# A hybrid attention/RWKV-7 layer on one core: the recurrence's chain in program order on TensorE, and 64-row products of two heads in turn

## The chip, the cores and the metric

The kernel runs on one core of a Trainium2 chip. The core has five engines with a queue of instructions each: TensorE (PE in the profile, its weight loads PEld), VectorE (DVE), ScalarE (ACT), GpSimd (POOL) and SyncE (SP, which here issues the DMAs). The metric is the device time of one execution in microseconds (us).

## The reference

The layer takes x of 1024 tokens by 1024 features. One projection of the normalised x feeds two mixers and a gate; the mixers' outputs are joined, gated, projected and normalised again.

```python
u = rmsnorm(h, norm_pre_g[l]);  p = u @ w_in[l]
p_mla, p_rw, z = jnp.split(p, [MLA_COLS, MLA_COLS + RW_SHIFT_COLS], axis=-1)
...                                   # MLA: 4 heads of causal attention, rope, low-rank q and kv -> y_mla
ps = p_rw + (token_shift(p_rw) - p_rw) * rw_mu[l]
r, k, v, xw, xa = jnp.split(ps, ...)  # 8 heads of 64 channels; xw, xa feed tanh/low-rank decay w and rate a
...
def step(S, inp):                     # one token; S is 64x64 per head
    r_t, w_t, k_t, v_t, kk_t, a_t = inp
    sa = jnp.einsum('bhvk,bhk->bhv', S, -kk_t)
    S = (S * w_t[:, :, None, :] + sa[..., None] * (kk_t * a_t)[:, :, None, :]
         + v_t[..., None] * k_t[:, :, None, :])
    return S, jnp.einsum('bhvk,bhk->bhv', S, r_t)
...                                   # group norm of y over each head, bonus -> y_rw
y_cat = jnp.concatenate([y_mla, y_rw], axis=-1) * jax.nn.silu(z)
h = h + rmsnorm(y_cat @ w_out[l], norm_post_g[l])
```

All of it is float32; projections are made of three products of split operands (a high part and a rest).

## The kernel before

**Stages.** A string, PROGRAM, names the stages in the order in which their instructions are created. The 1024 tokens are two halves (h = 0, 1) of 512. `A` loads x, normalises it and makes the transposed, split operand uH/uL (32 transposes of 128x128, L177, each group of four followed by two splits on ACT, L181, and two on DVE, L182). `X` projects the columns of the low-rank inputs (24 matmuls of 512 columns, L210), shifts, takes tanh and splits on DVE into xw and xa (L241 to L244). `P` makes k, r, v and decay of two heads (`P h cb`, cb = 0 to 3; its low-rank products are L250/L251), `E` the units of the chunked recurrence of these two heads, `I` the 64x64 inverses (four rounds of 32x32 products, L447 and L454, with DVE and DMA between), `C` the chain, `N` group norm, `G` the outputs. `Z` are blocks of the gate (24 matmuls of L210 each), `Y06` two of them at once in 96 matmuls of 256 columns; `M`, `T`, `U`, `K`, `J`, `Q` and `S` belong to the attention, `B` to the rope table (DVE, L655 to L676). In the order of PROGRAM, `A1 X1` (input of half 1) come behind the chain of half 0 and its outputs.

**What sets the order.** Each engine runs its queue in order. The queues are filled by a scheduler: it plays the instructions through a model of time, takes on each engine among those whose inputs are there, and gives way to the earlier in the program. So while the chain waits, instructions of later stages come between its steps. A tile taken from a pool holds back an instruction until the pool's oldest buffer is free; PSUM has pools `pj` (4 buffers), `wk` (2) and `ch` (2).

**Units.** A chunk is 64 tokens; a half has 8. Two heads lie on partitions 0 to 63 and 64 to 127. For each head (e = 0, 1) and four chunks, L359 multiplies 64 rows by 64 rows into 128x128 of a `wk` buffer; the same with a diagonal at L373, eight chunks into another `wk` buffer. A float32 matmul stands in the trace as two instructions. Before, `units` writes the L359 products with e as the inner loop, the L373 products head after head, and the scheduler sets the order on TensorE.

**The chain.** Eight steps, one a chunk, each of two groups g of two head pairs. Per group: L474 (four matmuls, eight instructions) state times LS; ACT copies the result out (L476); L480 four more into the same bank; L484 with AB; ACT and DVE copy it (L486, L487) into SV; L490 with BK; DVE adds the decayed state (L494, two of 64x128 a group), which is the state of the next step; L496 adds to the output, which ACT copies out (L499). In each, the four matmuls go over the quarters of the array.

**After the chain** `N` squares, reduces and takes a power on POOL (L510) per group, and `G` transposes the output by head (16 transposes of 64 rows a group, L525).

Of the kernel before, what the change touches and what calls it, by code (L numbers as in the profile page):

```python
# [44 lines left out]
def layer(tc, x, pos, w_in, w_out, w_uq, w_ukv, vecs, w2, a2, consts, post_g, out):  # L45
# [84 lines left out]
    "A0 X0 Z00 B P00 E00 Z01 P01 E01 Z02 P02 E02 P03 E03 I0 C0 N00 G00 N01 G01 M0 Z03 Z04 Z05 Y06 T0 A1 X1",  # L130
    "P10 E10 Z10 P11 E11 Z11 P12 E12 P13 E13 I1 C1 N10 G10 N11 G11 M1 Z12 T1 Z13 Z14 Z15 Z16 Z17 U K J Q0",
# [4 lines left out]
def recurrence(tc, E):  # L136
# [17 lines left out]
    def stage_a(h):

        XT = (("v", "sq"), ("sg", "cs"), ("a", "k"), ("kf", "r"))
        for pr in range(2):
            xs = []
            for q in range(2):
# [8 lines left out]
                E["rstd"](ss[:, 0:1], 1.0 / D)  # L168
# [3 lines left out]
            for k2 in range(4):  # L172
                ps = pj((128, 2, 256))
                for kk in range(2):
                    kb = k2 * 2 + kk
                    for q in range(2):
                        PE.transpose(ps[:, kk, q * 128:(q + 1) * 128], xs[q][kb // 4][:, (kb % 4) * 128:(kb % 4 + 1) * 128], ident)  # L177
                for kk in range(2):
                    kb = k2 * 2 + kk
                    sl = slice(pr * 256, pr * 256 + 256)  # L180
                    S.activation(uH[:, kb, sl], ps[:, kk], AF.Copy, scale=col(V_PRE + kb))  # L181
                    V.scalar_tensor_tensor(uL[:, kb, sl], ps[:, kk], col(V_PRE + kb),  # L182
                                           uH[:, kb, sl].bitcast(F32), ALU.mult, ALU.subtract)
# [19 lines left out]
    def proj(c0):  # L203
# [8 lines left out]
        return ps  # L212
# [22 lines left out]
    def lora_in(h):  # L235
        px = shifted(proj(CO_X), V_MU_X, "v", 1)
# [109 lines left out]
    def units(h, cb, gt, made):  # L346
# [6 lines left out]
        for c4 in range(0, NCH, 4):  # L353
            mk = mks[c4 // 4]
            pE = [wk((128, 4, 128)) for _ in range(2)]
            for ci in range(4):
                for e in range(2):
                    r = slice(e * 64, e * 64 + 64)
                    PE.matmul(pE[e][:, ci], pl[r, c4 + ci, 1 - e:3 - e].rearrange("p a b -> p (a b)"),  # L359
                              LS[r, c4 + ci, e, :], start=True, stop=True)  # L360
# [7 lines left out]
        G.tensor_tensor(dD, bc(id2.unsqueeze(1), (128, NCH, 64)), bc(Dg.unsqueeze(2), (128, NCH, 64)), ALU.mult)  # L368
        for e in range(2):
            r = slice(e * 64, e * 64 + 64)  # L370
            pB = wk((128, NCH, 64))
            for c in range(NCH):
                PE.matmul(pB[:, c], pl[r, c, 1 - e:3 - e].rearrange("p a b -> p (a b)"), dD[r, c], start=True, stop=True)  # L373
# [84 lines left out]
    def chain(h, gt):  # L458
# [4 lines left out]
        for c in range(NCH):  # L463

            pcs = [chp((128, 4, 2, 64)) for _ in range(2)]
            Rs = [alloc(P1, (128, 2, 64), "Rs", bufs=2) for _ in range(2)]
            SD = [alloc(P1, (128, 2, 64), "SD", bufs=2) for _ in range(2)]
            parts = []
            for g in range(2):
                LS, BK, AB, SV = (gt["g"][g][k] for k in ("LS", "BK", "AB", "SV"))  # L470
                parts.append((LS, BK, AB, SV, Sst[:, 2 * g:2 * g + 2], gt["Dg"][:, 2 * g:2 * g + 2], pcs[g], Rs[g], SD[g]))
            for LS, BK, AB, SV, St, Dg, pc, R_, D_ in parts:
                for l, e in le:
                    PE.matmul(pc[ev[e], 0, l], LS[:, l, c, e, 0:64], SV[:, c, e, l], start=(l == 0), stop=False,  # L474
                              skip_group_check=True)
                S.copy(R_, pc[:, 0])  # L476
                for e in range(2):
                    G.tensor_tensor(D_[ev[e]], SV[ev[e], c, e], bc(Dg[ev[e], :, c:c + 1], (64, 2, 64)), ALU.mult)  # L478
                for l, e in le:
                    PE.matmul(pc[ev[e], 1, l], LS[:, l, c, e, 64:128], SV[:, c, e, l], start=False, stop=False,  # L480
                              skip_group_check=True)
            for LS, BK, AB, SV, St, Dg, pc, R_, D_ in parts:
                for l, e in le:
                    PE.matmul(pc[ev[e], 2, l], AB[ev[e], l, c, 0:64], R_[ev[e], l], start=False, stop=False,  # L484
                              skip_group_check=True)
                S.copy(SV[ev[0], c, 0], pc[ev[0], 2])  # L486
                V.tensor_copy(SV[ev[1], c, 1], pc[ev[1], 2])  # L487
            for LS, BK, AB, SV, St, Dg, pc, R_, D_ in parts:
                for l, e in le:
# [571 lines left out]
```

## Time and profile before

| | |
|---|---|
| median of 3 runs | 786.29 us (783.88 to 789.08) |
| profiled execution, own time | 783.81 us |
| its span | 782.0 us |
| mean granted TensorE clock | 0.951 of full |
| DVE busy | 466.4 us (60%) |
| ACT busy | 347.9 us (44%) |
| POOL busy | 331.9 us (42%) |
| L210, all projections, busy | 215.7 us with uH, 130.2 us with uL |
| L359, busy, instructions | 35.6 us, 256 |
| L373, busy, instructions | 31.2 us, 256 |
| L525, busy, instructions | 4.2 us, 64 |

The table is read from the page's summary and from its groups. A matmul's time in a group includes its way through the array, so neighbours overlap: the time that a row of them takes is the distance of their starts. In timelines a row joins neighbours of one kind: start in us, length in us, engine, line, output and inputs, shape, count; a bracket gives the idle time of the engine ahead of it and who ended it. In windows, a row is a stretch: its length, busy time and count of each engine, the granted clock, the share of DMA and GB/s.

### The profile page before, as it was taken

How to read it: one execution, taken by the hardware profiler on the slowest of the kernel's cores; microseconds unless marked ns; L12 is line 12 of the kernel's file. 1: busy time of each engine (PE TensorE's matmuls, PEld its weight loads, DVE VectorE, ACT ScalarE, POOL GpSimd, SP SyncE). 2: the span in 40 equal slices, each digit the busy share in tenths (PEclk: the TensorE clock that was granted, in tenths of full speed). 3: DMA queues.
4: the chain of work that ended last, by engine and by line, in shares of the span. 5: the costliest groups of instructions: out<-in, count | busy, mean ns of one | idle time of the engine just before them, and what ended most of it. 6: DMA issues, size and time to landing. Idle time of an engine off the chain costs nothing. (4 is left out here: it accounts for less than half of the span.)

```text
span 782.0 us, 13855 instructions
## 1 busy us (share of the span) xinstructions
PE 713.0 (91%) x5136; PEld 586.1 (75%) x5136; DVE 466.4 (60%) x943; ACT 347.9 (44%) x877; POOL 331.9 (42%) x478
## 2 busy tenths in 40 slices
PE   2789999999978998889999989799899998899996
PEld 1667877789866776667888967577678997788885
DVE  4756757758925522495866691476497767644333
ACT  6465355343725453344353162426354566632221
POOL 6265645445942554263554374032332237442220
PEclk9999999999998899977999989879999999999999
DMA  6224241254383133043223366411023025144321
GB/s 208 80 69 115 54 114 51 68 151 134 114 187 89 28 108 83 2 89 85 57 68 97 86 171 156 131 44 42 2 55 101 21 89 162 52 166 141 121 82 54
DMA packets 118819, 72.84 MB, mean 93 GB/s; under 512 B 47072, under 2 KB 108256, under 8 KB 118752
## 3 DMA queue, kind: packets, MB, share of 16 engines
q1 hardware_dynamic: 118752, 71.96, 32.5%
q8 instruction: 40, 0.66, 0.4%
q14 instruction: 27, 0.22, 0.1%
HBM read 54.38 MB, written 17.56 MB: 92 GB/s over the span
## 5 line engine op out<-in xcount | busy, mean ns | idle before, releaser
L210 PE MATMUL pj<-uH,w 128*128 128x512 f32 x640 | 215.7, 411 | 3.3 <-DVE uL L182 2.5
L200 POOL TENSOR_TENSOR w<-wf,w 128x256 fp32r<-128x256 f32 x168 | 141.3, 871 | 116.6 <-ACT w L190 106.5
L210 PEld LDWEIGHTS pj<-uH,w 128*128 128x128 f32 x640 | 123.7, 195 | 33.1 <-DVE uL L182 2.9
L210 PE MATMUL pj<-uL,w 128*128 128x512 f32 x320 | 130.2, 407 | 0.0
L210 PEld LDWEIGHTS pj<-uL,w 128*128 128x128 f32 x320 | 62.6, 196 | 14.0 <-issue 0.8
L190 ACT CAST w<-wf 128x1024 fp32r<-128x1024 f32 (+1 forms) x50 | 51.4, 1027 | 28.8 <-PE pj L540 21.3
L478 POOL TENSOR_TENSOR SD<-SV,Dg 64x128 f32<-64x128 f32 x64 | 27.9, 436 | 74.0 <-DVE SV L494 59.9
L854 POOL TENSOR_SCALAR wf<-wf,sm 128x128 f32<-128x128 f32 (+7 forms) x32 | 24.0, 750 | 67.1 <-DVE sm L853 51.9
L198 POOL TENSOR_TENSOR w<-wf,w 128x224 fp32r<-128x224 f32 x32 | 23.8, 775 | 38.8 <-ACT w L190 32.2
L359 PEld LDWEIGHTS wk<-LS,pl 64*128 64x128 f32 x256 | 30.2, 191 | 12.5 <-issue 10.2
L979 DVE TENSOR_TENSOR LS<-pj,LS 128x512 f32<-128x512 f32 x16 | 11.1, 691 | 45.5 <-ACT cq L978 44.3
L359 PE MATMUL wk<-LS,pl 64*128 64x128 f32 x256 | 35.6, 289 | 1.3 <-DVE LS L317 1.2
L850 ACT ACTIVATE wf<-pj,mx 128x512 f32<-128x512 f32 (+3 forms) x48 | 27.7, 583 | 13.5 <-DVE mx L847 9.9
L865 ACT CAST BK<-wk 128x512 fp32r<-128x512 f32 (+3 forms) x48 | 22.4, 485 | 25.2 <-PE wk L863 23.2
L373 PEld LDWEIGHTS wk<-r,pl 64*128 64x128 f32 x256 | 29.5, 196 | 4.4 <-issue 2.9
L373 PE MATMUL wk<-r,pl 64*128 64x64 f32 x256 | 31.2, 284 | 1.2 <-DVE LS L364 1.0
L874 PE MATMUL ch<-BK,LS 128*128 128x256 f32 (+1 forms) x160 | 31.6, 282 | 0.7 <-ACT BK L865 0.7
L487 DVE COPY SV<-ch 64x128 f32<-64x128 f32 x32 | 9.2, 294 | 36.5 <-issue 25.7
L418 DVE TENSOR_TENSOR tmp<-XA 128x31 f32<-128x31 f32 (+15 forms) x62 | 28.2, 454 | 4.4 <-DMA XA<-sa 2.6
L866 DVE TENSOR_TENSOR AB<-wk,BK 128x512 fp32r<-128x512 f32 (+3 forms) x48 | 26.0, 551 | 7.3 <-ACT BK L865 6.8
L420 DVE TENSOR_TENSOR XA<-XA,tmp 128x31 f32<-128x31 f32 (+15 forms) x62 | 28.4, 458 | 1.9
L845 DVE TENSOR_REDUCE mx<-pj 128x1 f32<-128x512 f32 (+3 forms) x48 | 25.8, 551 | 6.0 <-PE pj L844 3.4
(339 smaller groups left out, 1659.4 us busy)
## 6 DMA issues: line engine op xcount, KB each, us to landing
wf<-in_w_in_dram SPq DMA_DIRECT2D x42, 512.0 KB, 3.9
zs<-st SPq DMA_DIRECT2D x16, 256.0 KB, 3.1
wf<-in_x_dram SPq DMA_DIRECT2D x8, 512.0 KB, 3.7
out_dram<-LS SPq DMA_DIRECT2D x16, 256.0 KB, 2.1
wf<-in_w_in_dram SPq DMA_DIRECT2D x8, 448.0 KB, 3.5
bvd<-st SPq DMA_DIRECT2D x8, 256.0 KB, 2.0
SV<-bvd SPq DMA_DIRECT2D x16, 128.0 KB, 3.4
yrw<-SV SPq DMA_DIRECT2D x8, 256.0 KB, 2.6
```

Of the source, the lines that this page charges most:

```text
L190: S.copy(wh, wf)
L200: G.tensor_tensor(wl[:, sl], wf[:, sl], wh[:, sl].bitcast(F32), ALU.subtract)
L210: PE.matmul(ps, w_[:, kb], u_[:, kb], start=(n == 0), stop=(n == 23))
L359: PE.matmul(pE[e][:, ci], pl[r, c4 + ci, 1 - e:3 - e].rearrange("p a b -> p (a b)"), LS[r, c4 + ci, e, :], start=True, stop=True)
L373: PE.matmul(pB[:, c], pl[r, c, 1 - e:3 - e].rearrange("p a b -> p (a b)"), dD[r, c], start=True, stop=True)
L418: V.tensor_tensor(t3, bc(At[:, j, j + 1:32].unsqueeze(2), (128, n, w)), bc(X[:, j, 0:w].unsqueeze(1), (128, n, w)), ALU.mult)
L420: V.tensor_tensor(X[:, j + 1:32, 0:w], X[:, j + 1:32, 0:w], t3, ALU.add)
L478: G.tensor_tensor(D_[ev[e]], SV[ev[e], c, e], bc(Dg[ev[e], :, c:c + 1], (64, 2, 64)), ALU.mult)
L845: V.tensor_reduce(mx[:, n5:n5 + 1], s_, axis=AX.X, op=ALU.min)
L850: S.activation(pr[:, b0:b1], sc[:, 0:b1 - b0], AF.Exp, bias=mx[:, 0:1], scale=-1.0, accum_out=sm[:, n5:n5 + 1])
L866: V.tensor_tensor(PL[:, b0:b0 + nb, o], pt[:, 0:nb], PH[:, b0:b0 + nb, o].bitcast(F32), ALU.subtract)
L874: PE.matmul(py[:, o], l_, r_, start=(j == 0 and n == 0), stop=(j == nk - 1 and n == 2), skip_group_check=True)
```

## The change

1. **Chain.** `chain` takes an iterator `fill`. Inside `tc.manual_schedule` TensorE keeps the program's order: the chain's blocks as written, group 0 before group 1, and one step of `fill` behind the two blocks with AB, one at the end of a step and one more at the end of every second. For half 0, `fill` is `stage_a(1)` and `lora_in(1)` cut into steps (eight of four transposes, then twelve of two matmuls); for half 1 it is empty. `A1 X1` go from PROGRAM.
2. **Order behind a mark.** `tc.issue_after` sets that what is created later on an engine also stands later in its queue: on DVE behind the last split of `A0`, on POOL behind its last power, on TensorE behind the last matmul of `C0`.
3. **64-row products.** In `units` the products of the two heads alternate matmul by matmul on TensorE (new L384, before L359; new L398, before L373, with both `wk` buffers taken at once); so do the transposes of `outputs` (new L558, before L525, two `ch` buffers at once).
4. **PROGRAM.** `M0 Z03 Z04 Z05 T0` move ahead of `C0`, `P10` ahead of `G00`, and `Y06` becomes `Z06 Z07` (48 matmuls of 512 columns).

Line numbers move: 170 to 182, 177 to 189, 181/182 to 194/195, 210 to 223, 250/251 to 274/275, 359 to 384, 373 to 398, 474 to 500, 480 to 506, 484 to 510, 490 to 517, 494 to 521, 496 to 523, 525 to 558, 655/661 to 700/706.

```diff
-        for op in " ".join(PROGRAM).split():
-            name = op.rstrip("0123456789")
-            ops[name](*(int(i) for i in op[len(name):]))
+        with contextlib.ExitStack() as order:
+            for op in " ".join(PROGRAM).split():
+                name = op.rstrip("0123456789")
+                last = ops[name](*(int(i) for i in op[len(name):]))
+                if op in ("A0", "C0"):
+                    for made in last:
+                        order.enter_context(tc.issue_after(made.ins))
...
-    "A0 X0 Z00 B P00 E00 Z01 P01 E01 Z02 P02 E02 P03 E03 I0 C0 N00 G00 N01 G01 M0 Z03 Z04 Z05 Y06 T0 A1 X1",
-    "P10 E10 Z10 P11 E11 Z11 P12 E12 P13 E13 I1 C1 N10 G10 N11 G11 M1 Z12 T1 Z13 Z14 Z15 Z16 Z17 U K J Q0",
+    "A0 X0 Z00 B P00 E00 Z01 P01 E01 Z02 P02 E02 P03 E03 I0 M0 Z03 Z04 Z05 Z06 Z07 T0 C0 N00 N01 P10 G00 G01",
+    "E10 Z10 P11 E11 Z11 P12 E12 P13 E13 I1 C1 N10 G10 N11 G11 M1 Z12 T1 Z13 Z14 Z15 Z16 Z17 U K J Q0",
...
+                if n % 2 == 0:
+                    yield
...
-            for ci in range(4):
-                for e in range(2):
-                    r = slice(e * 64, e * 64 + 64)
-                    PE.matmul(pE[e][:, ci], pl[r, c4 + ci, 1 - e:3 - e].rearrange("p a b -> p (a b)"),
-                              LS[r, c4 + ci, e, :], start=True, stop=True)
+            with tc.manual_schedule(engines={PE.engine}):
+                for ci in range(4):
+                    for e in range(2):
+                        PE.matmul(pE[e][:, ci], pl[ev[e], c4 + ci, 1 - e:3 - e].rearrange("p a b -> p (a b)"),
+                                  LS[ev[e], c4 + ci, e, :], start=True, stop=True)
...
+        pB = [wk((128, NCH, 64)) for _ in range(2)]
+        with tc.manual_schedule(engines={PE.engine}):
+            for c in range(NCH):
+                for e in range(2):
+                    PE.matmul(pB[e][:, c], pl[ev[e], c, 1 - e:3 - e].rearrange("p a b -> p (a b)"), dD[ev[e], c],
+                              start=True, stop=True)
...
-    def chain(h, gt):
+    def chain(h, gt, fill):
...
+        with tc.manual_schedule(engines={PE.engine}):
+            for c in range(NCH):
...
                 S.copy(SV[ev[0], c, 0], pc[ev[0], 2])
                 V.tensor_copy(SV[ev[1], c, 1], pc[ev[1], 2])
+                next(fill, None)
...
                 S.copy(SV[:, c, 0], pc[:, 1])
+                next(fill, None)
+                if c % 2:
+                    next(fill, None)
+            for _ in fill:
+                pass
+        return [mm]
...
+        pT = [chp((128, NCH, 64)) for _ in range(2)]
+        with tc.manual_schedule(engines={PE.engine}):
+            for c in range(NCH):
+                for e in range(2):
+                    PE.transpose(pT[e][:, c], SV[ev[e], c, 0].rearrange("p l v -> p (l v)"), ident[ev[e], ev[e]])
...
+    def op_c(h):
+        return chain(h, gts[h], itertools.chain(stage_a(1), lora_in(1)) if h == 0 else iter(()))
```

The first place is TensorE in a late step of the chain of half 0. Before (`ch` with two numbers are the PSUM tiles of the two groups):

```order
L474 MATMUL ch_2053<-SV_363,LS_360 64x64 x4
L474 MATMUL ch_2054<-SV_367,LS_364 64x64 x4
L480 MATMUL ch_2053<-SV_363,LS_360 64x64 x4
L484 MATMUL ch_2053<-Rs_2055,AB_362 64x64 x4
L480 MATMUL ch_2054<-SV_367,LS_364 64x64 x4
L484 MATMUL ch_2054<-Rs_2056,AB_366 64x64 x4
L490 MATMUL ch_2053<-SV_363,BK_361 64x64 x4
L490 MATMUL ch_2054<-SV_367,BK_365 64x64 x4
L496 MATMUL ch_2053<-SV_363,AB_362 64x64 x4
L496 MATMUL ch_2054<-SV_367,AB_366 64x64 x4
```

The same step in the changed kernel (the two `L223` rows are steps of `fill`, the projection of `X` for half 1):

```order
L500 MATMUL ch_2638<-SV_363,LS_360 64x64 x4
L506 MATMUL ch_2638<-SV_363,LS_360 64x64 x4
L500 MATMUL ch_2639<-SV_367,LS_364 64x64 x4
L506 MATMUL ch_2639<-SV_367,LS_364 64x64 x4
L510 MATMUL ch_2638<-Rs_2640,AB_362 64x64 x4
L510 MATMUL ch_2639<-Rs_2641,AB_366 64x64 x4
L223 MATMUL pj_2499<-uH_98,w_2493 128x512 x2
L517 MATMUL ch_2638<-SV_363,BK_361 64x64 x4
L523 MATMUL ch_2638<-SV_363,AB_362 64x64 x4
L517 MATMUL ch_2639<-SV_367,BK_365 64x64 x4
L523 MATMUL ch_2639<-SV_367,AB_366 64x64 x4
L223 MATMUL pj_2499<-uL_99,w_2493 128x512
```

Before, a block that waits for another engine's copy has a block of the other group ahead of it. Now the second and the fourth block of a group's turn stand directly behind the first and the third.

The second place is TensorE in `units` of the first two heads. Before:

```order
L210 MATMUL pj_514<-uH_98,w_508 128x512
L359 MATMUL wk_544<-LS_360,pl_431 128x128 x4
L384 MATMUL pj_598<-q_477,cst_64 128x512
L359 MATMUL wk_545<-LS_360,pl_431 128x128 x4
L210 MATMUL pj_620<-uH_98,w_614 128x512
```

And now (the two numbers of `wk` are the two heads; the first product, of `wk_544`, stands seven rows further up, alone between a projection and L411, before L384):

```order
L223 MATMUL pj_629<-uH_98,w_623 128x512
L384 MATMUL wk_545<-LS_360,pl_431 128x128
L384 MATMUL wk_544<-LS_360,pl_431 128x128
L384 MATMUL wk_545<-LS_360,pl_431 128x128
L384 MATMUL wk_544<-LS_360,pl_431 128x128
L384 MATMUL wk_545<-LS_360,pl_431 128x128
L384 MATMUL wk_544<-LS_360,pl_431 128x128
L384 MATMUL wk_545<-LS_360,pl_431 128x128
L223 MATMUL pj_629<-uH_98,w_623 128x512
```

Two rows of four products of one head have become seven products that change heads each time, and one that stands alone.

The third place is DVE at the start (`uL` is the split of `A0`, `posf` and `q` the rope table, `kf` and `r` two tiles of x). Before:

```order
L182 SCALAR_TENSOR_TENSOR uL_99<-pj_146,vec_65,uH_98 128x256
L661 TENSOR_SCALAR q_330<-cst_64,posf_327 128x32 x5
L170 TENSOR_SCALAR kf_178<-kf_178,ss_42_180 128x512
L170 TENSOR_SCALAR r_179<-r_179,ss_42_180 128x512
L661 TENSOR_SCALAR q_330<-cst_64,posf_327 128x32 x2
L182 SCALAR_TENSOR_TENSOR uL_99<-pj_155,vec_65,uH_98 128x256
```

And now, first where x's last tiles stand:

```order
L195 SCALAR_TENSOR_TENSOR uL_99<-pj_128,vec_65,uH_98 128x256
L195 SCALAR_TENSOR_TENSOR uL_99<-pj_137,vec_65,uH_98 128x256
L182 TENSOR_SCALAR kf_178<-kf_178,ss_42_180 128x512
L182 TENSOR_SCALAR r_179<-r_179,ss_42_180 128x512
L195 SCALAR_TENSOR_TENSOR uL_99<-pj_146,vec_65,uH_98 128x256
```

Then where the table begins:

```order
L195 SCALAR_TENSOR_TENSOR uL_99<-pj_201,vec_65,uH_98 128x256
L195 SCALAR_TENSOR_TENSOR uL_99<-pj_219,vec_65,uH_98 128x256
L195 SCALAR_TENSOR_TENSOR uL_99<-pj_210,vec_65,uH_98 128x256
L195 SCALAR_TENSOR_TENSOR uL_99<-pj_219,vec_65,uH_98 128x256
L700 CAST posf_327<-posi_325 128x8
L706 TENSOR_SCALAR q_330<-cst_64,posf_327 128x32 x8
```

The table's rows stood between x's last tiles and their splits, and stand behind all splits now.

More of the change, by code (lines that the diff above doesn't have):

```diff
@@ L1 @@
+import contextlib
+import itertools
 import math
@@ L57, in rstd @@
         G.tensor_scalar(ss, ss, scale, EPS, ALU.mult, ALU.add)
-        G.tensor_tensor(ss, ss, mhalf[:, 0:ss.shape[-1]], ALU.pow)
+        return G.tensor_tensor(ss, ss, mhalf[:, 0:ss.shape[-1]], ALU.pow)
     def bc(ap, shape):
@@ L149, in col @@
         return vec[:, c:c + 1]
+    ev = (slice(0, 64), slice(64, 128))
+    le = [(l, e) for l in range(2) for e in range(2)]
     uH = alloc(P1, (128, 8, HALF), "uH", F32R)
     uL = alloc(P1, (128, 8, HALF), "uL", F32R)
+    last = [None, None]
     def stage_a(h):
@@ L167, in stage_a @@
                 G.tensor_tensor(ss[:, 0:1], ss[:, 0:1], ss[:, 1:2], ALU.add)
-                E["rstd"](ss[:, 0:1], 1.0 / D)
+                last[1] = E["rstd"](ss[:, 0:1], 1.0 / D)
                 for i in range(2):
@@ L211, in proj @@
                 n += 1
-        return ps
+                if n % 2 == 0:
+                    yield
+        out.append(ps)
+    def proj(c0):
+        out = []
+        for _ in proj_steps(c0, out):
+            pass
+        return out[0]
     def shifted(ps, vi, tag, bufs):
@@ L235, in lora_in @@
     def lora_in(h):
-        px = shifted(proj(CO_X), V_MU_X, "v", 1)
+        out = []
+        yield from proj_steps(CO_X, out)
+        px = shifted(out[0], V_MU_X, "v", 1)
         th = alloc(P1, (128, 512), "sq")
@@ L462, in chain @@
                 G.tensor_copy(gt["g"][g]["SV"][ev[e], 0, e], Sst[ev[e], 2 * g:2 * g + 2])
[L463 to L489, printed above, removed]
-                    PE.matmul(pc[ev[e], 3, l], BK[:, l, c, e], SV[:, c, e, l], start=False, stop=False,
-                              skip_group_check=True)
-                for e in range(2):
-                    dst = SV[ev[e], c + 1, e] if c + 1 < NCH else St[ev[e]]
-                    V.tensor_tensor(dst, pc[ev[e], 3], D_[ev[e]], ALU.add)
-                for l, e in le:
-                    PE.matmul(pc[ev[e], 1, l], AB[ev[e], l, c, 64:128], SV[ev[e], c, e, l], start=False,
-                              stop=True, skip_group_check=True)
-                S.copy(SV[:, c, 0], pc[:, 1])
@@ L593, in recurrence, with run, op_a @@
     lora, xx, gts, cqs, made = {}, {}, {}, {}, {}
+    def run(*steps):
+        for _ in itertools.chain(*steps):
+            pass
+    def op_a(h):
+        run(stage_a(h))
+        return last
     def op_x(h):
-        if h == 0:
-            lora_load()
-        xx[h] = lora_in(h)
+        lora_load()
+        run(lora_in(h))
+    def op_c(h):
+        return chain(h, gts[h], itertools.chain(stage_a(1), lora_in(1)) if h == 0 else iter(()))
     def op_p(h, cb):
@@ L611, in recurrence @@
     return {
[L612 to L613 removed]
+        "A": op_a, "X": op_x, "P": op_p, "M": op_m, "T": lambda h: mla_tail(h, cqs[h]),
+        "E": op_e, "I": lambda h: inverse(h, gts[h]), "C": op_c,
         "N": lambda h, g: group_norm(h, g, gts[h]), "G": lambda h, g: outputs(h, g, gts[h]), "Z": lambda h, b: zgate(h, b, b + 1),
```

58 lines of the change are left out of this document (41 added, 17 removed).

## The prediction

> **What bounds the kernel now.** I read the page's summary first, then timelines of TensorE and of all engines in the stages that the change touches, and last TensorE's busy time in windows.
>
> ```profile
> PE 713.0 (91%) x5136; PEld 586.1 (75%) x5136; DVE 466.4 (60%) x943; ACT 347.9 (44%) x877; POOL 331.9 (42%) x478
> ```
>
> TensorE bounds: 713 of 782 us. So three things count: TensorE time taken away, its idle time, and its clock. That 91% is an average, though; the chain differs. This is a step of the chain of half 0 with nothing between its blocks (timeline of all engines, the chain's rows):
>
> ```profile
> 316.19 0.93 PE L474 MATMUL ch<-SV,LS 128*64 128x64 f32 x16
> 316.69 0.27 ACT L476 COPY Rs<-ch 128x128 f32<-128x128 f32 x1
> 317.01 0.45 PE L480 MATMUL ch<-SV,LS 128*64 128x64 f32 x8
> 317.39 0.45 PE L484 MATMUL ch<-Rs,AB 64*64 64x64 f32 x8
> ...
> 318.29 0.29 DVE L487 COPY SV<-ch 64x128 f32<-64x128 f32 x1 [2.53 <-issue]
> 318.64 0.45 PE L490 MATMUL ch<-SV,BK 128*64 128x64 f32 x8
> 319.38 1.21 DVE L494 TENSOR_TENSOR SV<-ch,SD 64x128 f32<-64x128 f32 x4
> 319.40 0.45 PE L490 MATMUL ch<-SV,BK 128*64 128x64 f32 x8 [0.31 <-DVE SV L487]
> 320.02 0.45 PE L496 MATMUL ch<-SV,AB 64*64 64x64 f32 x8 [0.17 <-DVE SV L494]
> 320.64 0.45 PE L496 MATMUL ch<-SV,AB 64*64 64x64 f32 x8 [0.17 <-DVE SV L494]
> 321.02 0.93 PE L474 MATMUL ch<-SV,LS 128*64 128x64 f32 x16
> ```
>
> A step takes 321.02 − 316.19 = 4.83 us. A block of eight instructions takes 317.39 − 317.01 = 0.38, ten of them 3.8, so about 1 us is waiting. The order of the two groups hides most of the copies: while ACT copies group 0's result, L474 of group 1 runs.
>
> **The chain's new order.** Four latencies matter. From L474's start to L480's of the same group, through the copy: 317.01 − 316.19 = 0.82. From L484 to L490 of group 0: 318.64 − 317.39 = 1.25. From L490 to L496: the adds begin 0.55 after it wherever DVE isn't late, two of them take 0.60, the start 0.04: 1.19 (in the rows above 1.38 for group 0, of which 0.2 is DVE's). The new order, block for block from 0: L500 of group 0 at 0, L506 at 0.82; group 1 at 1.20 and 2.02; L510 at 2.40 and 2.78; L517 of group 0 at 2.40 + 1.25 = 3.65, L523 at 4.84; group 1 at 5.22 and 6.41; the next step at 6.79. So the step takes 6.8 us instead of 4.83: L506 of group 0 now waits for its copy with L500 of group 1 queued behind it, L523 of group 0 waits for the add with L517 of group 1 behind. The steps of `fill` behind L510 lie in the 0.49 us before L517; those at a step's end lie on the path.
>
> **The clock.** Windows of 3.41 us (columns: stretch, its length, busy time and count of PE, PEld, DVE, ACT, POOL, granted clock, DMA):
>
> ```profile
> 251.48:254.90 3.42, 1.68 (x39) 1.40 (x40) 2.55 (x4) 2.56 (x9) 2.39 (x3) 1.00 0.00 0
> 254.90:258.31 3.41, 2.51 (x20) 1.92 (x17) 2.21 (x4) 0.81 (x3) 1.20 (x2) 0.50 0.30 61
> 258.31:261.72 3.41, 3.41 (x10) 2.64 (x9) 1.41 (x2) 3.18 (x5) 2.21 (x2) 0.50 0.32 97
> 306.09:309.50 3.41, 2.40 (x54) 1.79 (x48) 1.77 (x4) 1.67 (x7) 3.19 (x6) 1.00 0.03 7
> 323.16:326.57 3.41, 2.22 (x28) 1.96 (x28) 3.28 (x6) 2.01 (x6) 1.14 (x3) 1.00 0.02 5
> 326.57:329.98 3.41, 3.41 (x21) 2.33 (x20) 1.19 (x5) 0.57 (x1) 0.53 (x1) 0.50 0.00 0
> ```
>
> The grid is chosen so that the clock changes at its edges. After 1.68 and after 2.22 us of busy TensorE the next window is at half; after 2.40 it isn't (the step at 316, in the table above, has blocks of 0.38). At half, 2.51 did not bring the clock back. So I put the edge between 2.2 and 2.4 going down and above 2.5 coming up. The new bare step is busy for its 10 blocks and the tails of the five that a wait follows (0.07 each, 0.45 against 0.38), 4.15 us of 6.8, or 2.08 of 3.41: below the edge. At half clock a block takes 0.63:
>
> ```profile
> 503.44 0.69 PE L484 MATMUL ch<-Rs,AB 64*64 64x64 f32 x8
> 504.07 1.06 PE L728 MATMUL wk<-cst,k 128*64 128x128 f32 x4
> ```
>
> That is 0.25 more a block, and nine of them lie on the step's path: 9.04 us, with 10 × 0.63 and tails, 6.7, busy, or 2.54 a window: not enough to come back by the rows above. With `fill` the share is 64%, 2.2 a window.
>
> The Trainium skill ("TensorE: Matmul & The Clock Gate", section "Why this matters for your kernels") asks only that no idle gap of TensorE be over about 3 us. By it the chain, whose waits are all below 1 us, would keep full clock, and the sum would be that of the first rival. This trace speaks against it: the longest wait in the window 323.16 to 326.57 is 1.19, and half clock follows:
>
> ```profile
> 324.62 1.88 PE L359 MATMUL wk<-LS,pl 64*128 64x128 f32 x16 [1.19 <-DVE LS L317]
> ```
>
> **Half 0's chain, old and new.** Before, four steps lie between the projections of half 1 and cost their 3.8, four are bare: 4 × 3.8 + 4 × 4.83 = 34.5. `A1 X1` stand ahead and among them:
>
> ```profile
> 232.02 0.33 PE L177 MATMUL pj<-cst,v 128*128 128x128 f32 x1 [1.47 <-ACT st L565]
> ...
> 242.01 0.33 PE L177 MATMUL pj<-cst,k 128*128 128x128 f32 x1
> ...
> 242.60 0.45 PE L480 MATMUL ch<-SV,LS 128*64 128x64 f32 x8
> ...
> 244.32 0.62 PE L210 MATMUL pj<-uH,w 128*128 128x512 f32 x2
> 244.78 0.39 PE L210 MATMUL pj<-uL,w 128*128 128x512 f32 x1
> ...
> 256.70 0.79 PE L250 MATMUL pj<-xw,lora 128*128 128x512 f32 x1 [0.90 <-DVE xw L242]
> ```
>
> From the end of the work before (232.02 − 1.47) to 256.70 are 26.1 us; 6.1 of them are 16 blocks of the chain, 1.4 a row of L454: 18.6 for `A1 X1` with their waits. Together 53. New: eight steps of 6.8 are 54.4. Of the 20 steps of `fill`, 8 lie in the wait before L517; 12 are on the path: 4 of transposes at 242.60 − 242.01 = 0.59 and 8 of two matmuls at 2 × 0.23: 6. The eight splits' copies stand ahead of the chain's on ACT and DVE, by about one of 0.4 each: 3.3. That is 63.9 at full clock; at half, 9 × 0.25 a step and `fill` doubled, 88.4. I take half clock in six of the eight steps, 82: the first window must go by before the clock falls, and steps with three `fill` pieces may hold it.
>
> After the chain, before:
>
> ```profile
> 337.65 2.91 POOL L510 TENSOR_TENSOR gss<-gss,mhalf 128x16 f32<-128x16 f32 x1
> 338.49 5.81 PE L373 MATMUL wk<-r,pl 64*128 64x64 f32 x32 [1.04 <-DVE LS L364]
> 353.35 1.21 PE L525 MATMUL ch<-cst,SV 64*128 64x64 f32 x16 [4.14 <-DVE SV L513]
> ```
>
> The waits of 4.14, 1.04 and the 1.19 further up are 6.4, and the 32 products of L373 take 5.81 where they took 3.32 at full clock; with some 10 us that half clock costs over the stretch, 16 lost. New, all that is created after `C0` stands behind it. First comes L558, which waits for a copy, square, reduce, the power of 2.91 and two multiplies, 6.8 us by my estimate; then L274 waits for xw, whose splits share DVE with the group norm, until about 10.4; with a window of half clock behind, 12.4. So −4 (−12 to +4). Half 0 in all: 82 − 53 − 4 = +25 (full clock +7, half throughout +31).
>
> **Half 1's chain.** `fill` is empty; by the order of instructions four steps are bare and part of a fifth, before three. Full clock: 4 × 6.8 − 3 × 4.83 − 3.8 = 8.9, and 2 for the part: +11. Three of four at half clock, 2.2 each: +17.6. Attention's work follows at once and TensorE bounds it, so this lies on the path.
>
> **64-row products.** One head's L359 and L373, each with a row behind that gives its length:
>
> ```profile
> 63.55 1.16 PE L359 MATMUL wk<-LS,pl 64*128 64x128 f32 x8
> 64.64 1.12 PE L384 MATMUL pj<-q,cst 128*128 128x512 f32 x2
> ...
> 78.53 3.39 PE L373 MATMUL wk<-r,pl 64*128 64x64 f32 x32
> 81.85 0.72 PE L210 MATMUL pj<-uH,w 128*128 128x512 f32 x2
> ```
>
> 8 take 1.09, 32 take 3.32: 0.104 each. Where the trace has by chance two heads in turn, the starts are 0.05 apart, for one of each head:
>
> ```profile
> 371.77 0.27 PE L359 MATMUL wk<-LS,pl 64*128 64x128 f32 x1
> 371.82 0.27 PE L373 MATMUL wk<-r,pl 64*128 64x64 f32 x1
> ```
>
> So the halves overlap. L359, 256 instructions in 28 pieces: 32.7 us; in turn, 13 pieces of 1 and 7 products and three of 8, at 0.104 alone and about 0.055 in turn, 22.6: −10. L373: 28, to eight pieces of 1 and 15, 2.36 each, 18.9: −9. L525: −1. That is −20 on TensorE, which has no gap in these stages (columns as in the windows above):
>
> ```profile
> 395.00:430.00 35.00, 35.00 (x192) 28.46 (x191) 24.82 (x37) 13.30 (x34) 17.43 (x23) 1.00 0.28 79
> ```
>
> DVE works 24.8 of 35 us there, so a period 2.5 shorter still leaves it time; but `wk` has two buffers and both heads now hold them at once, so I take −17. The bounds are −22 and, if those few rows don't carry over to whole pieces, +3 for the changes of half. `Y06` in two has as many columns in half the instructions; 48 × 0.23 = 11 us and no row says that 96 shorter ones took much more: −0.5 (−1 to 0).
>
> **Start.** The table's rows on DVE lie between x and its splits:
>
> ```profile
> 17.00 3.64 DVE L661 TENSOR_SCALAR q<-cst,posf 128x32 f32<-128x32 f32 x5
> 26.90 0.80 PE L210 MATMUL pj<-uH,w 128*128 128x512 f32 x1 [2.54 <-DVE uL L182]
> 43.63 0.77 PE L250 MATMUL pj<-xw,lora 128*128 128x512 f32 x1 [2.61 <-DVE xw L242]
> ```
>
> Without them the last tiles are scaled 3.6 us earlier and the splits run without gaps. The table then stands ahead of the shift and of xw's splits, which still have to wait for 24 matmuls. I take −4.5 (0 to −6).
>
> **Sum.** 783.8 (own time) − 4.5 − 17 − 0.5 + 25 + 17.6 = 804.4. The median before lies 2.5 above the profiled execution; with it 807. Changes of about 1% (778.4 to 794.2) are what a measurement can tell from none.
>
> **Rivals.** (1) *The clock holds* in both chains, since the waits are short: half 0 +7, half 1 +11, and the sum is 779.8, with the 2.5 782. For it: 2.2 of 3.41 in the steps with `fill` is on the edge. Against: 1.68 and 2.22 were followed by half. A chance of 0.25. (2) *Faster: DVE's late starts vanish.* L487 began 0.35 after TensorE's block was done, by "issue" and no wait, L494 0.29 after; with the groups apart each copy finds an idle DVE. Then a step is 6.79 − 0.35 − 2 × 0.29 = 5.86; busy 2.4 a window, so the clock holds too; half 0 gives 63.9 − 8 × 0.93 − 57 = −0.5, half 1 11 − 5 × 0.93 = 6.4; with all 20 of the products: 783.8 − 4.5 − 20 − 0.5 − 0.5 + 6.4 = 764.7, with the 2.5 767. It decides from a step of about 6.2, where the share passes 2.3. 0.20. (3) *The halves don't overlap* in the written pieces: +3 for −17, 827. 0.05. The forecast keeps 0.50.
>
> **Range.** The forecast alone has 794 to 822 (half clock in fewer steps; all of them, and products at −12). Down to 770 it takes in the first rival and some of the second: outside are 0.15 of that and the third's 0.05. Faster by over 1%: the second, and a fifth of the first, 0.25; within: the rest of the first, some of the forecast's foot, 0.24; slower 0.51.
>
> **What would show it.** Right: rows of L506 and L523 with waits for ACT and DVE, some 0.4 and 0.8 each; windows of half clock across both chains; L398's 0.05 apart; the first L223 before 23 us; the distance of first to last chain row near 82 us in half 0. Wrong: bare steps under 6 us, a clock of 1.00 through the chain, or stalls of `fill` on PSUM or ACT that make its steps longer than 11 us.

## The result and the profile after

The changed kernel takes 821.6 us (median of 4 runs, 813.1 to 826.9) against 785.1 before. The ratio leaves out two of these runs, which were slower at a lower clock, and so is not the quotient of the medians: it is 1.038, with an interval of 1.029 to 1.048. The prediction was 807 us, 770 to 822, slower with a chance of 0.51. The direction and its main reason were right. The measured time stands at the upper end of the range, though: the profiled execution took 817.5 us where the sum without the added 2.5 has 804.4, so about 13 us are missing.

The page's summary of the kernel after, and the rows of its 40 slices for TensorE and its clock:

```profile
PE 704.6 (86%) x5088; PEld 572.8 (70%) x5088; DVE 462.1 (57%) x943; ACT 350.6 (43%) x876; POOL 332.7 (41%) x478
...
PE   3899998999467777999999988597788999899996
...
PEclk9899999999855695999999999697579999999998
```

TensorE has 8 us less busy time in its records and 42 us more idle time (815.7 − 704.6 against 782.0 − 713.0). Two stretches stand out: slices 11 to 16 (from about 204 to 326 us) and 26 to 30 (510 to 612). They are the inverse and the chain of half 0, and those of half 1.

Where the time came in is best read from a few marks, start or end of rows in the timelines of TensorE (us from the span's start):

| | before | after | after − before |
|---|---|---|---|
| first low-rank product (L250, now L274) | 43.6 | 37.2 | −6.4 |
| last product of E03 (L359, now L384) | 172.2 | 168.8 | −3.4 |
| chain of half 0 starts | 236.8 | 236.8 | 0 |
| chain of half 1 starts | 500.1 | 519.2 | +19.1 |
| chain of half 1 ends | 576.8 | 612.5 | +35.7 |
| end | 782.0 | 815.7 | +33.7 |

The start brought TensorE forward by 6.4 us; at the last product of E03 3.4 of it are left, and at the chain of half 0 nothing. From there to the start of half 1's chain the kernel loses 19 us, and in that chain 17; behind it 2 come back.

A step of half 1's chain with nothing between its blocks (timeline of TensorE, kernel after):

```profile
576.00 0.69 PE L500 MATMUL ch<-SV,LS 128*64 128x64 f32 x8
577.06 0.69 PE L506 MATMUL ch<-SV,LS 128*64 128x64 f32 x8 [0.36 <-ACT Rs L502]
577.54 0.64 PE L500 MATMUL ch<-SV,LS 128*64 128x64 f32 x8
578.54 0.69 PE L506 MATMUL ch<-SV,LS 128*64 128x64 f32 x8 [0.36 <-ACT Rs L502]
579.17 1.12 PE L510 MATMUL ch<-Rs,AB 64*64 64x64 f32 x16
580.66 0.69 PE L517 MATMUL ch<-SV,BK 128*64 128x64 f32 x8 [0.37 <-DVE SV L513]
582.04 0.69 PE L523 MATMUL ch<-SV,AB 64*64 64x64 f32 x8 [0.69 <-DVE SV L521]
582.66 0.69 PE L517 MATMUL ch<-SV,BK 128*64 128x64 f32 x8
584.05 0.69 PE L523 MATMUL ch<-SV,AB 64*64 64x64 f32 x8 [0.69 <-DVE SV L521]
584.67 0.69 PE L500 MATMUL ch<-SV,LS 128*64 128x64 f32 x8
```

It takes 584.67 − 576.00 = 8.67 us, where a step before took 4.83. Five waits of 0.36 to 0.69 stand in it, each ahead of a block whose input another engine is still copying. And each block takes 0.63 (579.17 − 578.54) instead of 0.38: TensorE runs at half clock. Windows of 3.41 us of half 0's chain (columns as in the prediction):

```profile
261.69:265.10 3.41, 3.19 (x36) 2.43 (x34) 0.89 (x3) 0.99 (x3) 0.00 (x0) 0.50 0.03 5
265.10:268.51 3.41, 1.98 (x25) 1.56 (x25) 1.73 (x6) 0.74 (x2) 1.29 (x4) 0.50 0.00 0
...
271.93:275.34 3.41, 3.28 (x36) 2.66 (x36) 0.59 (x2) 1.05 (x4) 0.00 (x0) 0.50 0.00 0
275.34:278.75 3.41, 1.76 (x30) 1.31 (x27) 2.71 (x7) 1.66 (x6) 1.43 (x4) 1.00 0.00 0
278.75:282.17 3.42, 3.06 (x28) 1.95 (x26) 0.69 (x1) 0.89 (x2) 0.16 (x1) 0.50 0.02 5
282.17:285.58 3.41, 2.35 (x43) 1.70 (x42) 1.10 (x4) 0.76 (x3) 0.14 (x1) 1.00 0.00 0
...
299.24:302.66 3.42, 2.03 (x34) 1.45 (x34) 1.21 (x5) 0.53 (x2) 1.48 (x4) 1.00 0.00 0
302.66:306.07 3.41, 2.68 (x34) 1.95 (x32) 0.00 (x0) 0.53 (x2) 0.11 (x1) 0.50 0.02 5
```

1.76 and 2.03 us of busy TensorE are followed by half clock, 3.28 and 3.06 by full. No single bound on the busy time sorts all windows, though: 3.19 at half clock, with blocks and four transposes as in the window with 3.28, is followed by half, and in half 1's chain 2.08 at full clock is followed by full, 2.15 by half (TensorE alone):

```profile
548.41:551.82 3.41, 2.08 (x28) 1.00 0.33 98
551.82:555.23 3.41, 3.41 (x45) 1.00 0.44 126
...
558.65:562.06 3.41, 2.15 (x48) 1.00 0.00 0
562.06:565.47 3.41, 2.36 (x38) 0.50 0.00 0
```

Over the whole chain the mean clock is 0.66, in half 1's 0.75 (windows, TensorE alone, the second stretch half 1):

```profile
237.00:312.50 75.50, 57.42 (x693) 0.66 0.04 10
...
519.00:612.50 93.50, 76.47 (x845) 0.75 0.08 22
```

What happened ahead of the chain is in the inverse. The stretch from 178 to 237 us, before and then after (windows of TensorE, each a row of its own kernel):

```profile
178.00:237.00 59.00, 52.86 (x526) 0.95 0.57 149
```

```profile
178.00:237.00 59.00, 40.06 (x417) 0.83 0.52 134
```

After, TensorE is busy 13 us less there, and the row where that shows is a wait for a DMA of the inverse:

```profile
225.84 0.31 PE L471 MATMUL ch<-XA,AB 32*32 32x32 f32 x2 [12.33 <-DMA XA<-sx]
```

All other work that was ready is done by then: `M0`, the gates and `T0` came sooner, and the transposes of `A1`, which stood in these waits before, have moved into the chain. The clock fell to half in this gap, so the chain began at half clock (windows of TensorE):

```profile
213.90:217.31 3.41, 0.00 (x0) 1.00 0.00 0
217.31:220.73 3.42, 0.00 (x0) 0.50 0.83 293
```

### The profile page after: what moved, and what is told of

Its sections match the earlier page's. It is cut to its first block, busy times and chain, and to the rows that moved or that the text cites. A ratio compares the mean times of both kernels' runs of the same rounds, so it can differ in the third digit from the quotient of the medians.

```text
span 815.7 us, 13749 instructions
## 1 busy us (share of the span) xinstructions
PE 704.6 (86%) x5088; PEld 572.8 (70%) x5088; DVE 462.1 (57%) x943; ACT 350.6 (43%) x876; POOL 332.7 (41%) x478
## 5 line engine op out<-in xcount | busy, mean ns | idle before, releaser
L223 PE MATMUL pj<-uH,w 128*128 128x512 f32 x672 | 227.4, 412 | 7.0 <-ACT sg L301 4.5
L213 POOL TENSOR_TENSOR w<-wf,w 128x256 fp32r<-128x256 f32 x168 | 143.5, 884 | 103.6 <-ACT w L203 91.5
L223 PEld LDWEIGHTS pj<-uH,w 128*128 128x128 f32 x672 | 128.7, 194 | 38.2 <-ACT sg L301 4.9
L223 PE MATMUL pj<-uL,w 128*128 128x512 f32 x336 | 136.0, 405 | 0.0
L223 PEld LDWEIGHTS pj<-uL,w 128*128 128x128 f32 x336 | 65.4, 195 | 14.7 <-issue 1.0
L442 DVE TENSOR_TENSOR tmp<-XA 128x31 f32<-128x31 f32 (+15 forms) x62 | 29.0, 468 | 15.2 <-DMA XA<-sa 13.4
L523 PE MATMUL ch<-SV,AB 64*64 64x64 f32 x256 | 18.2, 277 | 20.3 <-DVE SV L521 18.9
L523 PEld LDWEIGHTS ch<-SV,AB 64*64 64x64 f32 x256 | 13.0, 172 | 25.8 <-DVE SV L521 23.3
L526 ACT COPY SV<-ch 128x128 f32<-128x128 f32 x32 | 8.6, 268 | 48.8 <-PE ch L523 48.8
L506 PE MATMUL ch<-SV,LS 128*64 128x64 f32 x256 | 19.3, 293 | 10.5 <-ACT Rs L502 10.5
```

What stands on the lines that cost most here:

```text
L213: G.tensor_tensor(wl[:, sl], wf[:, sl], wh[:, sl].bitcast(F32), ALU.subtract)
L223: PE.matmul(ps, w_[:, kb], u_[:, kb], start=(n == 0), stop=(n == 23))
L442: V.tensor_tensor(t3, bc(At[:, j, j + 1:32].unsqueeze(2), (128, n, w)), bc(X[:, j, 0:w].unsqueeze(1), (128, n, w)), ALU.mult)
L523: mm = PE.matmul(pc[ev[e], 1, l], AB[ev[e], l, c, 64:128], SV[ev[e], c, e, l], start=False, stop=True, skip_group_check=True)
```

## The experiments

Each ratio is to the kernel before, with its interval. The marks are taken from the trace as in the table above. Two theories are followed: A, the prediction's sum (TensorE's time and clock decide, so what it is spared comes off the end), and B, formed from the trace after (ahead of the inverse another path decides, so spared time becomes idle time).

**1. Products in turn, alone.** The kernel before with the hunks of `units` and `outputs` of the change and nothing else:

```diff
+        pB = [wk((128, NCH, 64)) for _ in range(2)]
+        with tc.manual_schedule(engines={PE.engine}):
+            for c in range(NCH):
+                for e in range(2):
```

> The kernel before with one part of the change alone: the 64-row products of the two heads (and the output transposes) in turn. Theory A (the prediction's): TensorE bounds these stages, so the time that the overlap frees comes off the end: about -17 us, ratio 0.978. Theory B (from the trace after): the recurrence's own path over VectorE, ScalarE and the DMAs of the inverse sets when the chain starts, and TensorE time freed ahead of it turns into idle time there: the chain of half 0 starts within 3 us of 236.8 as before, the idle time of TensorE ahead of the chain grows, and the end moves by 0 to -6 us, ratio 0.992 to 1.00.

Ratio 1.016 (1.010 to 1.023): slower, outside both ranges. TensorE's busy time fell as forecast, by 18.7 us:

```profile
PE 694.3 (88%) x5136; PEld 566.0 (72%) x5136; DVE 463.2 (59%) x943; ACT 350.1 (44%) x877; POOL 328.3 (41%) x478
```

But the chain of half 0 starts at 245.1, 8.3 us later. VectorE's row for the last products of E03 shows a first part of it:

```profile
171.95 0.68 DVE L367 TENSOR_TENSOR AB<-wk,cs 64x512 f32<-64x512 f32 x1 [5.07 <-PE wk L363]
```

Before, the two waits for these products were 1.03 and 1.29 us. With the heads in turn, both `wk` buffers are needed before a piece can run, so the next piece waits until VectorE has read both. That is the smaller part: VectorE begins the inverse 2.1 us later than before (180.99 against 178.88). The larger part stands directly ahead of the chain, where transposes of `A1` and six products of `X` at half clock are in TensorE's queue between the last products of the inverse (L458, until 238.3) and the chain's first block (timeline of TensorE):

```profile
238.27 0.47 PE L180 MATMUL pj<-cst,a 128*128 128x128 f32 x1
...
242.22 0.80 PE L213 MATMUL pj<-uH,w 128*128 128x512 f32 x1 [1.14 <-ACT st L571]
...
245.09 1.12 PE L478 MATMUL ch<-SV,LS 128*64 128x64 f32 x16
```

These are 6.8 us; before, that stretch was 1.6 (from 235.2 to 236.8). Theory A's step falls. Of B, the idle time holds: from 178 to 236.8 us TensorE is busy 47.7 us where it was 52.7. But B had the chain start within 3 us of 236.8 and the end no later than before, and both failed.

**2. The mark behind A0, alone.** The kernel before, with

```diff
+                if op == "A0":
+                    for made in last:
+                        order.enter_context(tc.issue_after(made.ins))
```

> The kernel before with the mark behind A0 alone (VectorE's rope table behind all splits, GpSimd's work behind the last power). Theory A: the first low-rank product moves from 43.6 to about 37 us and that carries to the end: -4.5 to -6.4 us, ratio 0.992 to 0.994. Theory B: that product moves as far, but the start of the chain of half 0 moves by less than 3 us and the end by 0 to -3 us.

Ratio 0.997 (0.994 to 1.000). The first low-rank product comes at 36.6 us (−7.0) and half 0's chain starts at 231.9 (−4.9), so here the path does carry most of it: B is wrong on the chain's start. The chain of half 1 starts 5.4 us earlier and yet ends at 577.5, 0.8 later, in the profiled run: the gain goes in the interleaved work of that chain. By the end it is worth 3 us (0.4 to 5), which is B's 0 to 3 and less than A's 4.5, though the interval doesn't exclude A.

**3. The chain's order, alone.** The kernel before with the chain's blocks in program order, without steps of other work:

```diff
+        with tc.manual_schedule(engines={PE.engine}):
+            for c in range(NCH):
```

> The kernel before with the chain's blocks alone in program order on TensorE (group 0 ahead of group 1, second block behind the first of the same group), no steps of other work, A1 X1 where they were. Theory A (the order of the blocks makes the step 6.8 us at full clock and 8.7 at half): half 1 +16 us as in the trace after, half 0's bare steps +8 to +15: 24 to 31 us slower, ratio 1.03 to 1.04. Rival (the loss comes from A1 X1 moved into the chain and out of the inverse's waits): not over +16 us in all, ratio at most 1.02.

Ratio 1.048 (1.044 to 1.051): the order of the blocks alone costs about as much as the whole change (1.038), or somewhat more. Half 0's chain ends 21 us later than before, half 1's takes 96.9 us instead of 76.7. The rival falls; theory A's size was too low.

**4. The groups in turn.** The changed kernel, still in program order and with the steps of `fill`, but the blocks as the scheduler had them:

```diff
-                for LS, BK, AB, SV, St, Dg, pc, R_, D_ in parts:
+                first(*parts[0])
+                first(*parts[1])
+                second(*parts[0])
+                third(*parts[0])
+                second(*parts[1])
+                third(*parts[1])
```

(`first`, `second` and `third` are L500, L506 and L510 with their copies; L517 of both groups likewise stands ahead of L523 of both.)

> The changed kernel, its chain still in program order with the named steps of other work, but the blocks written with the two groups in turn: L500 of both, L506 and L510 of group 0, L506 and L510 of group 1, L517 of both, L523 of both. Theory A (the order of the blocks is what costs): bare steps of half 1 at about 4.9 us and full clock instead of 8.7 at half, that chain 16 us shorter; the chain of half 0 50 to 57 us instead of 75.6; in all -32 to -42 us against the changed kernel, about 0.985 to 1.0 of the kernel before. Rival (program order as such and the steps of other work cost): half 0's chain stays over 65 us and the whole stays at least 10 us over the kernel before.

Ratio 0.990 (0.986 to 0.993): 4.7% less than the changed kernel (0.990 over 1.038), and faster than before. Half 0's chain takes 52.3 us instead of 75.6, half 1's 77.1 instead of 93.3, both as expected. So neither program order nor the steps of other work cost; the order of the two groups does. One part of the expectation failed: the bare steps of half 1 are at half clock here too (windows, TensorE alone, and the timeline of a step):

```profile
545.98:549.39 3.41, 3.41 (x50) 0.50 0.02 5
549.39:552.81 3.42, 3.18 (x44) 0.50 0.00 0
552.81:556.22 3.41, 3.41 (x50) 0.50 0.00 0
```

```profile
545.97 1.17 PE L500 MATMUL ch<-SV,LS 128*64 128x64 f32 x16
...
550.39 0.70 PE L527 MATMUL ch<-SV,BK 128*64 128x64 f32 x8 [0.17 <-DVE SV L516]
...
552.40 1.17 PE L500 MATMUL ch<-SV,LS 128*64 128x64 f32 x16
```

A step there takes 6.43 us, with a single wait of 0.17.

**5. The fourth without the alternation.** As experiment 4, with `units` and `outputs` as before.

> The kernel of the fourth experiment (changed kernel, the chain's groups in turn) with the 64-row products and output transposes as before, head after head. Theory B (the alternation holds both wk buffers at once, so the products of the next piece wait for VectorE and the inverse starts late): the chain of half 0 starts at 230 to 233 us instead of 236.8, and the whole is 4 to 10 us faster than the fourth experiment, ratio 0.977 to 0.985 to the kernel before. Theory A (freed TensorE time counts): 10 us or more slower than it, ratio over 1.00.

Ratio 0.988 (0.982 to 0.993), not to be told from experiment 4. The chain of half 0 starts at 233.3, 3.5 us earlier, close to B's 230 to 233, but the time doesn't show B's 4 to 10 us. A's 10 us or more are excluded. Half 1 tells the same: from its first low-rank product to its chain the profiled run takes 197.3 us (296.6 to 493.9) without the alternation and 198.6 (296.4 to 495.0) with it, in experiment 4.

**6. Work in the waits.** The changed kernel with products of no use in the chain's waits:

```diff
+                idle = pj()
...
+                    for _ in range(1):
+                        PE.matmul(idle[:, 0:128], ident, ident, start=True, stop=True)
```

(one ahead of each L506, two ahead of each L523).

> The changed kernel with extra products of no use (128x128 by 128 columns into a spare PSUM tile, six in a step of the chain) placed in the waits ahead of L506 (one each) and L523 (two each); they take work added, some 1.3 us of TensorE a step, and leave nothing out. Theory A (the clock follows the busy share of a window of 3.41 us): windows of the chain go to full clock, the bare steps of half 1 fall from 8.7 to 6.8 to 7.3 us and half 0's chain from 75.6 to 62 to 68 us: 12 to 20 us faster than the changed kernel, ratio 1.012 to 1.023. Rival (only an idle gap of about 3 us lowers the clock, or the block order alone costs): no faster, and up to 8 us slower.

Ratio 1.093 (1.087 to 1.100): far slower, as neither said. The chains themselves went as theory A forecast: half 0's took 62.2 us, and the bare steps of half 1 run at full clock with the work added (timeline, then a window of them; L505 and L526 are the added rows):

```profile
500.38 0.45 PE L501 MATMUL ch<-SV,LS 128*64 128x64 f32 x8
500.76 0.49 PE L505 MATMUL pj<-cst 128*128 128x128 f32 x2
501.20 0.45 PE L509 MATMUL ch<-SV,LS 128*64 128x64 f32 x8
...
504.26 0.71 PE L526 MATMUL pj<-cst 128*128 128x128 f32 x4
505.02 0.45 PE L528 MATMUL ch<-SV,AB 64*64 64x64 f32 x8
...
506.92 0.45 PE L501 MATMUL ch<-SV,LS 128*64 128x64 f32 x8
```

```profile
506.83:510.24 3.41, 3.02 (x58) 2.34 (x54) 0.17 (x1) 1.29 (x5) 0.60 (x2) 1.00 0.00 0
```

6.54 us instead of 8.67, with more to do. The loss lies elsewhere: between the steps of half 1's chain, which starts at 484 and ends at 550 us, stand only 49 products of `M1` (the attention's input) where the changed kernel has 205 instructions of the attention, and that work and the last gates come behind it, with gaps. Behind the chain TensorE takes 304.5 us, where it took 203.2 (window of TensorE alone):

```profile
600.00:650.00 50.00, 34.37 (x197) 0.83 0.25 74
```

The spare tiles come from the pool `pj`, which that work needs too; that they hold it back is argued, not shown by a wait. Experiment 10 leaves them out of half 1, and the 205 instructions stand in its chain again.

**7. Two pools for the products.** Experiment 4, the second head's products in the pool `ch`, which is idle at that time:

```diff
-            pE = [wk((128, 4, 128)) for _ in range(2)]
+            pE = [wk((128, 4, 128)), chp((128, 4, 128))]
...
-        pB = [wk((128, NCH, 64)) for _ in range(2)]
+        pB = [wk((128, NCH, 64)), chp((128, NCH, 64))]
```

> The kernel of the fourth experiment, with the products of the second head in buffers of the pool ch, which is idle then, and those of the first in wk: each head has two buffers again. Theory B (lockstep on two wk buffers takes the gain of the alternation): VectorE's waits for L384 before the last products of E03 fall under 2 us, the products of E03 end 3 us or more earlier, and the whole is 4 to 12 us faster than the fourth experiment, ratio 0.975 to 0.985. Rival (the buffers don't matter; the alternation's gain is lost at the inverse in any case): within 3 us of the fourth experiment, ratio 0.986 to 0.994.

Ratio 0.979 (0.975 to 0.983). The last product of E03 ends at 153.0 instead of 169.5 us, VectorE's waits of 5 us for the products are gone, and half 0's chain starts at 230.3. The lockstep was there, and without it the alternation pays in this kernel: 767.0 us against 775.3 in experiment 5, which leaves it out, some 8 us.

**8. The transposes of A1 early.** Experiment 5 with `A1` ahead of `C0` in PROGRAM and only `lora_in(1)` as `fill`.

> As the fifth experiment, but the 32 transposes of A1 ahead of C0 in the program, where they can fill the waits of the inverse; only the projection of X is left as steps within the chain. Theory (the hole of 12 us that A1's removal left in the inverse costs the clock and the time that the transposes then take in the chain): half 0's chain 5 to 8 us shorter than in the fifth experiment, its start not later by more than 2, the whole 3 to 8 us faster than it. Rival (the inverse's end is not moved and the chain hides the transposes): within 2 us, or slower where transposes stand ahead of the inverse's own products.

Ratio 0.991 (0.987 to 0.995), against 0.988: no gain. Half 0's chain takes 58.5 us against 56.1, not less; transposes still stand between its first blocks.

**9. Two pools, alone.** Experiment 1 with the pools of experiment 7.

> The kernel before with the alternation of the two heads alone, as in the first experiment, but the second head's products in the pool ch, so that each head has two buffers. Theory B (the alternation costs because both heads share two wk buffers): VectorE no longer waits 5 us for the products ahead of the inverse, the chain of half 0 starts at 228 to 234 instead of 245 us, and the whole is 6 to 14 us faster than the kernel before, ratio 0.982 to 0.992. Rival (the alternation gains nothing by itself; what the seventh experiment gained came from the chain): ratio 0.997 or more.

Ratio 1.002 (0.999 to 1.005). The loss of experiment 1 is gone, so it came with the two shared buffers. But there is no gain, and the ratio is the rival's: theory B's size fails. (The rival's other half, that experiment 7 gained by the chain alone, doesn't hold: experiment 5 has the same chain and gains less.) The products of E03 end at 154.7 us, 17.5 earlier than before, and the chain of half 0 still starts at 236.2. Of the 17.5 us, 8 are left where VectorE begins the inverse (170.8 us against 178.9) and 0.6 at the chain; some of them are lost directly ahead of it (timeline of TensorE):

```profile
233.47 0.47 PE L180 MATMUL pj<-cst,v 128*128 128x128 f32 x1 [3.41 <-ACT st L571]
...
236.22 0.73 PE L478 MATMUL ch<-SV,LS 128*64 128x64 f32 x16
```

Transposes of `A1` stand ahead of the chain's first block in TensorE's queue and wait 3.41 us for ScalarE. In experiment 7, where they stand in the chain, it starts at 230.3.

**10. Work in the waits of half 0 only.** Experiment 6, its products left out of half 1's chain.

> The changed kernel with the extra products in the waits of half 0's chain only, so that half 1's chain keeps its interleaved work. Theory A (the clock follows TensorE's busy share): half 0's chain takes 61 to 65 us instead of 75.6, half 1's stays at 93, and the whole is 9 to 15 us faster than the changed kernel, ratio 1.019 to 1.028. Rival (time gained there is lost again at the inverse of half 1): ratio over 1.033.

Ratio 1.020 (1.014 to 1.025), inside the range: half 0's chain takes 62.2 us instead of 75.6, half 1's 95.9, and useless work makes the changed kernel 1.8% faster. In the chain the mean clock is 0.95 where it was 0.66:

```profile
237.20:299.40 62.20, 59.88 (x789) 0.95 0.03 9
```

**11. Two pools and A1 early.** Experiment 7 with `A1` ahead of `C0`.

> The kernel of the seventh experiment with the transposes of A1 ahead of C0, where they can stand in the waits of the inverse. Theory (the hole ahead of the inverse is wider now that the products end earlier, so filling it pays): 3 to 8 us faster than the seventh experiment, ratio 0.968 to 0.975. Rival (as the eighth experiment showed against the fifth, it makes no difference): ratio 0.976 to 0.982.

Ratio 0.972 (0.968 to 0.976): the fastest of all, 765.1 us. Against experiment 7 (0.979, 0.975 to 0.983) the intervals touch and the medians are 1.9 us apart (767.0 there), so that the step from 7 to 11 is worth something is possible, not shown.

**12. The changed kernel without the alternation.** `units` and `outputs` as before, all else changed.

> The changed kernel with one part undone: the 64-row products and the output transposes head after head as before. The prediction's step (the alternation takes 17 us off): 17 us slower than the changed kernel, ratio about 1.06 to the kernel before. Theory B (what the alternation frees of TensorE becomes idle time ahead of the inverse, and the lockstep of the two wk buffers delays it): the chain of half 0 starts 3 to 5 us earlier than 236.8, and the whole is 0 to 6 us faster than the changed kernel, ratio 1.030 to 1.040.

Ratio 1.036 (1.031 to 1.042) against 1.038 with it. Half 0's chain starts at 231.4 us, 5.4 earlier (the profiled execution took 828.8 us against a median of 817.5, so only what lies ahead of the chains is read from it). The wait of 12.33 us in the inverse is 3.73 here:

```profile
217.49 0.31 PE L468 MATMUL ch<-XA,AB 32*32 32x32 f32 x2 [3.73 <-DMA XA<-sx]
```

In the changed kernel, then, the alternation is worth nothing that can be told from none (the intervals leave some 8 us either way), and not 17 us.

## Why the prediction was right, and where the sum failed

- **The chain's new order: right.** The waits stand where the prediction put them, and their sizes are near: L506 0.36, L523 0.69 (it said 0.4 and 0.8). The step without clock loss is 6.54 us (experiment 6, with the added products in the waits; forecast 6.8), at half clock 8.67 (forecast 9.04). Experiments 3 and 4 show the order as the cause.
- **The clock: right in this kernel, with another start.** Half 0's chain runs two thirds of its time at half clock (mean 0.66), half 1's half of it (0.75). Of the 23.3 us that half 0's chain takes more than in experiment 4, 13.4 go when the waits are filled (experiment 10) and about 10 stay with the waits. But the clock first fell not within the chain, as "the first window must go by before the clock falls" has it, but in the wait of 12.33 us ahead of it; within the chain it came back at 275 us and fell again at 279 and 303. The edge "between 2.2 and 2.4 going down and above 2.5 coming up" is not one: 2.08 held full clock, 2.15 lost it, and 3.19 at half did not bring it back. The first rival, that the clock holds because the waits are short, does not hold: half 1's chain went to half clock at 562 us behind a window whose longest wait is 0.69 us. The Trainium skill ("TensorE: Matmul & The Clock Gate", section "Why this matters for your kernels") asks that TensorE have no idle gap over about 3 us between bursts. The wait of 12.33 us agrees with it, and in half 1's chain keeping to it was not enough.
- **Half 0's chain: 75.6 us, forecast 82; what follows it: 7.1 us to the next low-rank product, forecast 10.4.** Both were priced too high, by 6.4 and 3.3 us. From the chain's start to that of half 1's the kernel lost 19.1 us, and the prediction has +25 and −8.5, half of the products' gain, in that stretch: 16.5. That these are near is luck, since the 8.5 were not there (experiments 5 and 12).
- **Half 1's chain: 16.6 us longer (93.3 against 76.7), forecast 17.6.**
- **"That is −20 on TensorE … so I take −17": the step that failed.** On TensorE it was right: 18.7 us less busy in experiment 1, and the pieces are shorter (in the kernel after, a piece of 30 takes 1.92 us where 32 took 3.32):

```profile
457.35 2.00 PE L398 MATMUL wk<-r,pl 64*128 64x64 f32 x30
...
459.27 0.48 PE L573 MATMUL pj<-w,uH 128*128 128x448 f32 x1
```

  But "no gap in these stages" doesn't mean that spared time comes off the end. TensorE had no gap because other work filled it; with fewer products that work was done sooner, and the wait for the inverse took what was spared: 12.33 us in the changed kernel, 3.73 without the alternation (experiment 12). The prediction named `wk`'s two buffers and priced them at 3 us; by themselves they cost about 11 (experiment 1 against 9: 1.016 and 1.002). Without that cost the 17 don't appear either: nothing alone (experiment 9), some 8 us with the chain's groups in turn (7 against 5).
- **The start: −4.5 taken, −6.4 at the first low-rank product, 0 at the chain in the changed kernel.** By itself it carries to the chain (experiment 2) and is worth 3 us at the end; in the changed kernel it went the way of the products.
- **How near the sum came is partly luck.** It has +20.6 us, and 33.7 were measured between the spans of the two profiled runs. Gains of 22 (17, 4.5 and 0.5 of the gates) did not show in the changed kernel. Against them the losses were priced too high: half 0's chain by 6.4, what follows it by 3.3, half 1's chain by 1.0; and 2.0 came back behind it. These make 12.7, so that about 9 of the 13.1 us missing are traced to terms of the sum; the rest is open.

What stays open: why the gain of experiment 2 is lost in half 1's chain, and why experiment 8 gains nothing (its first low-rank product of half 1 comes at 291.0 us, 5.6 earlier than in experiment 5) where 11 may.

## What to carry to other kernels

Ask of spared time on a full engine what fills its place: if what fills it is work that only waits its turn, the end moves only when the path through the other engines moves too. When two products share the array in turn, give each its own pair of buffers, or the pipelining with the reader is lost. In a chain of short dependent blocks, put a block of another group between a block and the one that waits for its copy; it saves the wait. Whether it also keeps the clock has to be looked at: in experiment 4 it did in half 0's chain (1.00 from 249 us to its end) and did not in the bare steps of half 1's.

## What was not expected of the hardware

- Work of no use in the waits of a chain made the kernel faster (experiment 10 against the changed kernel: 1.020 against 1.038), since the clock rose from a mean of 0.66 to 0.95 there.
- TensorE's recorded busy time doesn't decide the clock alone. In experiment 4, windows with 3.41 and 3.18 of 3.41 us busy with 64-row blocks at half clock did not bring it back in over 20 us, where in the kernel after 3.06 and 3.28, with transposes or 512-column products among the blocks, did, and 3.19 with transposes did not. The records of neighbouring small products overlap (0.45 us long at starts 0.38 apart), so that busy time in records need not be the array's work; which measure decides was not settled.
